# Weight loads of an attention layer put on ScalarE's DMA queue, the filling of three heads changed, and a bank of its own for the last half product

## The chip, the cores and the metric

The kernel runs on one core of one Trainium2 chip. The metric is the device time of one execution in microseconds (us). The number to compare is the median of several executions; the profile is taken from one execution more.

## The reference

The program is a streaming encoder trunk: attention, MLP, a gated linear recurrence, MLP, each with an RMSNorm ahead and a residual add behind, and a last RMSNorm. There are 512 tokens of 1024 channels, all in float32. What the change touches is the attention and the last lines of the last MLP and norm:

```python
qkv = jnp.einsum('bsd,de->bse', h, w_qkv).reshape(B, S, 3, N_HEADS, HEAD_DIM)
...
s = jnp.einsum('bqhd,bkhd->bhqk', q_c, k_band).astype(jnp.float32) * scale + bias
s = jnp.where(key_pos[None, None, None, :] >= 0, s, NEG_INF)
p = jax.nn.softmax(s, axis=-1).astype(v_band.dtype)
return jnp.einsum('bhqk,bkhd->bqhd', p, v_band)
...
return jnp.einsum('bsd,de->bse', o, w_o)
```

There are 16 heads of 64 channels, a band of nine chunks of 64 tokens, and a learned bias by clipped distance. With 512 tokens the band is all earlier tokens and the own chunk.

## The kernel before, in words

**Number format.** Every float32 product is made of three matmuls: high by high, high by low and low by high (`mm3`, L287 to L290). So every operand is split into a high part, a rounded copy, and a low part, the difference.

**Weight units.** Weights come in units of 512 KB, in the order of a list called `plan`. For a unit of the attention, `fetch` (L138) does three things in a row: the DMA into a raw buffer `wr` (L154), the cast of the high part `wh` on ScalarE (ACT, L179), and the subtraction for the low part `wl` on VectorE (DVE, L184). There are three raw buffers, `wr0` to `wr2`, so the DMA of a unit waits until the subtraction of the unit three places earlier has read its buffer. There are five buffers each for `wh` and `wl`. The DMAs stand on SyncE's (SP) queue; only one half of the very first unit is on ACT's. The units are: 0 to 5 for the query and key columns of the heads 0 to 3 (`FIRST`), 6 to 9 for the values of the heads 0 to 7, 10 to 17 for four further pairs of heads, 18 to 21 for the other values, 22 to 25 for the last two pairs, 26 to 33 for the output projection. The MLP's first unit is 34 (`starts[0]`). `want` keeps four units ahead.

**Order of the attention.** Six units of query and key products come first, and among them `flat` (L328): the sum of squares for the norm is cast (`n0a`, L331), summed over the partitions by two matmuls with ones (`n0ss`, L333 and L334) and turned into a scale `n0r` (L336). After that comes a loop over the heads (L674). Each pass holds the scores of head i (`score`, L473: eight matmuls L483 and L484, four passes of the bias and the maximum on DVE L491, four exponentials on ACT L498), the split of the probabilities of head i-2 (`split_p`: `pH` on ACT L549, `pL` on DVE L550), the weighing with the values of head i-3 (`weigh`: matmuls L567 and L568 into the bank `oa`, a copy `ax` on ACT L573, an add `o` on DVE L574), and the division of head i (`divide`: ACT L515, a transpose on DVE L517, and 16 small DMAs L521 that move the blocks `p`, 6 on SP's queue and 10 on GpSimd's, POOL). Four PSUM banks serve scores and `oa` in turn (three for the scores of a head, one for `oa`), so a `weigh` also waits until the maxima of the latest scores have been read. The k parts of a pair of heads go through SP's queue too (L400), and so does each head's bias (L374).

**Filling.** Twice in a pass `fill(n)` puts other TensorE (PE) work between these steps: value products, query and key products of later pairs, and the output projection `wo`. It takes matmuls by a credit of `n`: `FILL` is 11.7 for the heads 0 to 12 and `LATE` is 6.0 after them. What is left is run behind the last head.

**The end.** In `ends` (L1083) the last of the Strassen products, "22", is formed in two parts: `ts=(0,)` into the bank `X[0]`, and `ts=(1,)` into the bank `X[1]`, in two halves of 256 columns, LO and HI. After LO, `X[1]` is read by DVE (L1118), then HI's matmuls follow into the same bank, and DVE reads again. Squares, roots, scales and stores of the rows follow piece by piece (L1094 to L1134).

Of the kernel before, what the change touches and what calls it, by code (L numbers as in the profile page):

```python
# [10 lines left out]
F32 = mybir.dt.float32  # L11
F32R = mybir.dt.float32r
AF = mybir.ActivationFunctionType
ALU = mybir.AluOpType

P = 128
# [3 lines left out]
NH = 16  # L20
# [2 lines left out]
EPS = 1e-6  # L23
NEG = -1e30

FILL, LATE, TURNED = 11.7, 6.0, NH - 2

WARM = 10

# [11 lines left out]
def trunk(ctx: ExitStack, tc: tile.TileContext, xT, cols, gfin, win, wqkv, wo, rwin, rga, rgx, rwo, w1, w2, out):  # L41
    nc = tc.nc
# [9 lines left out]
    def mmp(name):  # L52
        return ps.tile([P, T], F32, name=name, tag="mm")
# [45 lines left out]
    plan = []  # L99
# [9 lines left out]
    def rows(src):  # L109
        return src.rearrange("(k p) c -> p k c", p=P)  # L110
# [14 lines left out]
    def load_up(key, name):  # L125
# [9 lines left out]
        if name == "s1":  # L135
            G.dma_start(four(raw), rows(upper[key]["22"]), accum_op=ALU.add)  # L136

    def fetch():  # L138
        i = state["next"]
        state["next"] += 1  # L140
        kind, nk, key = plan[i]
        H = wsp.tile([P, 1024], F32R, name=f"wh{i}", tag="wh")
        L = wsp.tile([P, 1024], F32R, name=f"wl{i}", tag="wl")
        n, half = 1024, nk
        if kind[:5] == "plain":
            n = nk * sum(src.shape[1] for src in key)
            raw = wraw.tile([P, 1024], F32, name=f"wr{i}", tag=f"wr{state['plain'] % 3}")
            state["plain"] += 1
            rv = raw[:, :n].rearrange("p (k c) -> p k c", k=nk)
            c0 = 0  # L150
            for n_, src in enumerate(key):
                w = src.shape[1]
                queue = nc.scalar if i == 0 and n_ else nc.sync
                queue.dma_start(rv[:, :, c0 : c0 + w], rows(src))  # L154
                c0 += w
        elif kind[0] == "u":
            nk = 4
            following = (key[0], key[1] + 1)
            if kind == "us2":
                raws["us2"] = wraw.tile([P, 1024], F32, name=f"us2_{key[0]}{key[1]}", tag=f"wr{(state['base'] + 2) % 3}")  # L160
                tc.keep_in_program_order(V.tensor_add(raws["us2"], raws["u11"], raws["us1"]))
                raws["us3"] = raws["u11"]
                G.dma_start(four(raws["us3"]), rows(upper[key]["21"]), accum_op=ALU.add)  # L163
            if kind == "us4":
                raws["us4"] = raws["u12"]
                V.tensor_add(raws["us4"], raws["us4"], raws["us2"])
            raw = raws[kind]
        else:
            nk = 2
            following = (key[0], key[1] + 1)  # L170
            raw = raws[{"t1": "12", "t2": "22", "t3": "11", "t4": "21"}.get(kind, kind), half]
            if kind == "t2":
                if key[1] < 3:
                    V.tensor_add(raw, raw, raws["12", half])
                G.dma_start(raws["21", half], raw, accum_op=ALU.add)
            if kind == "t3" and key[1] < 3:
                V.tensor_sub(raw, raws["22", half], raw)
        if i:
            high = S.copy(H[:, :n], raw[:, :n])  # L179
            if kind in ("us1", "us3", "t1", "t4") or kind in ("t2", "t3") and key[1] == 3:  # L180
                tc.keep_in_program_order(high)
        else:
            start_.append(V.tensor_copy(H[:, :n], raw[:, :n]))
        low = V.tensor_sub(L[:, :n], raw[:, :n], f(H[:, :n]))  # L184
        if not i:
            start_.append(low)
        if kind == "plain_":
            state["base"] = state["plain"] % 3
            load_up((nk_layer[i], 0), "11")
            load_up((nk_layer[i], 0), "12")  # L190
        elif kind == "us2" and key[1]:
            load_up(following, "s1")
        elif kind == "us3":
            load_up(following, "11")
        elif kind == "us4":
            load_up(following, "12")
        elif kind == "u22" and key[1]:
            load_up(following, "22")
        elif kind in ("11", "t1", "22", "21", "t2", "t3", "t4") and key[1] == 3:
            hs = slice(half * U, (half + 1) * U)  # L200
            if kind == "t1":
                nc.sync.dma_start(two(raws["11", half]), rows(down[key]["22"][hs]))
                G.dma_start(two(raws["11", half]), rows(down[key]["12"][hs]), accum_op=ALU.add)
            elif kind == "22":
                G.dma_start(raws["22", half], raws["12", half], accum_op=ALU.add)
        elif kind == "t2" and half:
            load_down(following, "12")
        elif kind == "t3" and half:
            load_down(following, "11")
        elif kind == "t4" and half:  # L210
            first_sum(following)
            load_down(following, "22")
            load_down(following, "21")
        state["ready"].append((nk, H[:, :n].rearrange("p (k c) -> p k c", k=nk), L[:, :n].rearrange("p (k c) -> p k c", k=nk)))
# [150 lines left out]
    with ExitStack() as actx:  # L365
# [268 lines left out]
        def step():  # L634
            for item in list(queue):
                if item[0][0] not in "qkv" and item is not queue[0]:
                    break
                try:
                    n = next(item[1])
                except StopIteration:  # L640
                    queue.remove(item)
                    return True
                if n:
                    credit[0] -= n
                    return True
            return False
# [25 lines left out]
            at["w"] = h  # L672

        for i in range(NH + 2):  # L674
            n = FILL if i < 13 else LATE
            if i < NH:
                if 0 < i < NH - 2:
                    bias_of(i + 2)
                if i >= 4:
                    need(f"q{i // 2}")  # L680
                score(i)
                if i == 0:
                    k_out(1, accs[3])
                at["s"] = i
            fill(n)
            if 0 <= i - 2 < NH - 2:
                split_p(i - 2)
            if 0 <= i - 3 < NH - 2:
                weigh_at(i - 3)
            fill(n)  # L690
            if i < NH:
                divide(i)
            if i >= NH:
                split_p(i - 2)
                fill(n)
                weigh_at(i - 2)
# [41 lines left out]
    def mlp(ly, norm):  # L738
        with ExitStack() as mctx:
# [73 lines left out]

            def read(acc, t, c):
                d, r = dt[t, c], (nrq if c else rq)[:, t : t + 1]
                V.scalar_tensor_tensor(d, acc, r, d, ALU.mult, ALU.add)


            a = {}
# [263 lines left out]
            def ends(step, product, X, gfins):  # L1083
                gain = [gfins[:, c] for c in range(2)]

                def store(t, c, queue):
                    queue.dma_start(out[t * P : (t + 1) * P, c * T : (c + 1) * T], dt[t, c])

                tc.keep_in_program_order(S.activation(spare, epsb, AF.Sqrt))
                step("s3", X, False, 2, 1)  # L1090
                for t in range(2):
                    for c in range(2):
                        squares(t, c)
                    V.tensor_add(total(t), total(t), part(t, 1))  # L1094
                    S.activation(total(t), total(t), AF.Sqrt, bias=epsb, scale=1.0 / D)
                    V.reciprocal(total(t), total(t))
                    for c in range(2):
                        V.scalar_tensor_tensor(dt[t, c], dt[t, c], total(t), gain[c], ALU.mult, ALU.mult)
                        store(t, c, nc.sync)
                for t in (2, 3):  # L1100
                    squares(t, 1)
                    V.tensor_scalar(part(t, 1), part(t, 1), 1.0 / D, EPS, ALU.mult, ALU.add)
                    V.tensor_mul(dt[t, 1], dt[t, 1], gain[1])
                product("22", X, False, ts=(0,))
                read(X[0], 2, 0)
                squares(2, 0)
                S.activation(total(2), total(2), AF.Sqrt, bias=part(2, 1), scale=1.0 / D)
                V.reciprocal(total(2), total(2))
# [2 lines left out]
                S.activation(dt[2, 1], dt[2, 1], AF.Copy, scale=total(2))  # L1111
                store(2, 1, nc.scalar)

                d, x, g = dt[3, 0], X[1], gain[0]
                sq = wk.tile([P, T], F32, name="fsq30", tag="nsq", bufs=2)
                for n, c in enumerate((LO, HI)):
                    product("22", X, False, ts=(1,), cols_=c)
                    V.scalar_tensor_tensor(d[:, c], x[:, c], rq[:, 3:4], d[:, c], ALU.mult, ALU.add)  # L1118
                    S.activation(sq[:, c], d[:, c], AF.Square, accum_out=fs[:, 4 * n : 4 * n + 1])
                    if n == 0:  # L1120
                        V.scalar_tensor_tensor(part(3, 1), fs[:, 0:1], 1.0 / D, part(3, 1), ALU.mult, ALU.add)
                        V.tensor_mul(d[:, c], d[:, c], g[:, c])
# [221 lines left out]
```

## Time and profile before

| | |
|---|---|
| median of three executions | 1023.05 us (1020.48 to 1025.93) |
| the profiled execution | 1022.14 us, of which the profile's span is 1020.3 us |
| PE busy | 1005.4 us (99%) |
| DVE busy | 858.2 us (84%) |
| ACT busy | 681.6 us (67%) |
| POOL busy | 170.7 us (17%) |
| largest wait of PE for another engine | 4.5 us, at 185.81 us |
| attention, first score (L483) to last weighing (L568) | 41 to 219 us |

A page of the profile lists the busy time of each engine, its share of the span and its count of instructions. In a row of the timeline stand the start, the duration, the engine, the line, the operation, the tiles as out<-in, shapes and how many; in square brackets stands how long the engine was idle ahead of it, and which instruction released it. PE's matmuls overlap, so their spacing is the difference of two starts. "SPq" is a DMA issue on SP's queue. Of a matmul that stands in a row behind another, the duration is longer than the spacing.

### The profile page before, as it was taken

Reading aid. Unit: us, or ns where it says so; the run is one execution under the profiler, and the core shown is the slowest. Engines: PE = TensorE matmul, PEld = TensorE weight load, DVE = VectorE, ACT = ScalarE, POOL = GpSimd, SP = SyncE. Lnnn points to the kernel's source line nnn. Section 1 sums busy time; section 2 is a strip of 40 time slices with the busy share of each in tenths; the row PEclk is TensorE's granted clock in tenths of the full one; section 3 lists DMA queues with packets and bytes.
Section 4 is the critical chain, followed back from the end, with each engine's and each line's share of the span. In section 5 each row is a group of like instructions: output and inputs, shape, how many; then the busy total and the mean of one; then the engine's idle time right before and its main releaser. Section 6 shows DMA issues by size and latency. Waiting matters only on the chain.

```text
span 1020.3 us, 15680 instructions
## 1 busy us (share of the span) xinstructions
PE 1005.4 (99%) x5650; PEld 880.3 (86%) x5650; DVE 858.2 (84%) x1136; ACT 681.6 (67%) x1032; POOL 170.7 (17%) x280
## 2 busy tenths in 40 slices
PE   9999999899999999999999999999999999999997
PEld 8888888688999999999988788888999999999986
DVE  7798888889799798698698988977699698798687
ACT  7577787656876566576477696546776566566565
POOL 1055454404011011011110000013011111111020
PEclk9999999899999999999999999999999999999999
DMA  8687768648757657746863313196748747737572
GB/s 267 170 236 195 188 172 227 191 136 215 207 128 197 171 131 177 188 105 165 228 121 109 119 63 97 49 277 157 206 86 205 205 83 207 206 63 207 145 153 95
DMA packets 136749, 167.03 MB, mean 164 GB/s; under 512 B 10784, under 2 KB 101536, under 8 KB 136672
## 3 DMA queue, kind: packets, MB, share of 16 engines
q1 hardware_dynamic: 109536, 121.83, 38.8%
q0 software_dynamic: 26560, 43.50, 23.3%
q8 instruction: 44, 0.72, 0.3%
q10 hardware_dynamic: 576, 0.72, 0.2%
q14 instruction: 33, 0.27, 0.1%
HBM read 123.27 MB, written 2.10 MB: 123 GB/s over the span
## 4 chain that ended last, share of the span: by engine, by line
PE 77%; DVE 8%; DMA 5%; ACT 4%; issue 3%; SPq 2%; POOL 1%; DVEq 0%; ACTq 0%
PE m L290 9%; PE m L289 9%; PE m L288 9%; PE x L289 5%; PE x L288 5%; PE x L290 5%; PE y L288 4%; PE y L289 4%; PE y L290 4%; DVE wl L184 2%; DMA wr<-in_wqkv 2%; DMA p<-pt 2%; PE ro L290 1%; PE yb L288 1%; PE ro L289 1%
## 5 line engine op out<-in xcount | busy, mean ns | idle before, releaser
L184 DVE TENSOR_TENSOR wl<-b,wh 128x1024 fp32r<-128x1024 f32 x112 | 135.8, 1222 | 37.2 <-ACT wh L179 37.1
L179 ACT CAST wh<-b 128x1024 fp32r<-128x1024 f32 x112 | 116.9, 1051 | 63.4 <-PE m L289 19.9
L290 PE MATMUL m<-rH,wl 128*128 128x256 f32 x448 | 125.9, 281 | 0.0
L289 PE MATMUL m<-rL,wh 128*128 128x256 f32 x448 | 125.8, 281 | 0.0
L288 PE MATMUL m<-rH,wh 128*128 128x256 f32 x448 | 125.7, 281 | 0.0
L290 PE MATMUL m<-hnH,wl 128*128 128x256 f32 x336 | 95.0, 283 | 0.0
L289 PE MATMUL m<-hnL,wh 128*128 128x256 f32 x336 | 95.0, 283 | 0.0
L288 PE MATMUL m<-hnH,wh 128*128 128x256 f32 x336 | 94.9, 282 | 0.0
L179 ACT CAST wh<-wr 128x1024 fp32r<-128x1024 f32 (+1 forms) x65 | 66.6, 1028 | 36.7 <-PE ro L289 8.5
L184 DVE TENSOR_TENSOR wl<-wr,wh 128x1024 fp32r<-128x1024 f32 (+1 forms) x66 | 78.3, 1191 | 12.3 <-ACT wh L179 11.9
L289 PEld LDWEIGHTS m<-rL,wh 128*128 128x128 f32 x448 | 85.0, 190 | 1.2
L288 PEld LDWEIGHTS m<-rH,wh 128*128 128x128 f32 x448 | 84.8, 189 | 1.0
L290 PEld LDWEIGHTS m<-rH,wl 128*128 128x128 f32 x448 | 84.9, 189 | 0.0
L521 POOL DMA_DIRECT2D p<-pt x140 | 68.7, 499 | 58.0 <-DVE pt L517 34.6
L179 ACT CAST wh<-u 128x1024 fp32r<-128x1024 f32 x56 | 58.2, 1051 | 28.0 <-PE x L290 16.9
L184 DVE TENSOR_TENSOR wl<-u,wh 128x1024 fp32r<-128x1024 f32 x56 | 67.6, 1219 | 2.3 <-ACT wh L179 2.3
L289 PEld LDWEIGHTS m<-hnL,wh 128*128 128x128 f32 x336 | 64.3, 191 | 0.8
L288 PEld LDWEIGHTS m<-hnH,wh 128*128 128x128 f32 x336 | 64.2, 191 | 0.8
L290 PEld LDWEIGHTS m<-hnH,wl 128*128 128x128 f32 x336 | 64.3, 191 | 0.0
L136 POOL DMA_DIRECT2D kept<-in_w x14 | 18.3, 1306 | 272.9 <-DVE t L1284 146.6
L163 POOL DMA_DIRECT2D u<-in_w x14 | 18.4, 1315 | 229.1 <-ACT m L906 122.3
L288 PE MATMUL x<-wh,h 128*128 128x512 f32 (+1 forms) x132 | 51.0, 386 | 0.6 <-DVE d L1118 0.6
(389 smaller groups left out, 2998.9 us busy)
## 6 DMA issues: line engine op xcount, KB each, us to landing
b<-in_w SPq DMA_DIRECT2D x68, 512.0 KB, 5.9
b<-b POOLq DMA_DIRECT2D x36, 512.0 KB, 6.7
kept<-in_w SPq DMA_DIRECT2D x28, 512.0 KB, 4.2
u<-in_w SPq DMA_DIRECT2D x28, 512.0 KB, 6.2
wr<-in_wqkv SPq DMA_DIRECT2D x20, 512.0 KB, 4.8
wr<-in_rwin SPq DMA_DIRECT2D x16, 512.0 KB, 3.7
kept<-in_w POOLq DMA_DIRECT2D x14, 512.0 KB, 6.9
u<-in_w POOLq DMA_DIRECT2D x14, 512.0 KB, 7.7
```

The source lines that it names most:

```text
L136: G.dma_start(four(raw), rows(upper[key]["22"]), accum_op=ALU.add)
L163: G.dma_start(four(raws["us3"]), rows(upper[key]["21"]), accum_op=ALU.add)
L179: high = S.copy(H[:, :n], raw[:, :n])
L184: low = V.tensor_sub(L[:, :n], raw[:, :n], f(H[:, :n]))
L288: PE.matmul(acc, WH, XH, start=start, stop=False, skip_group_check=more)
L289: PE.matmul(acc, WH, XL, start=False, stop=False, skip_group_check=more)
L290: PE.matmul(acc, WL, XH, start=False, stop=stop, skip_group_check=more)
L521: move = queue.dma_start(pt[32 * j : 32 * j + 32, i * 320 : (i + 1) * 320], turned[32 * i : 32 * i + 32, j].rearrange("p s a -> p (s a)"),)
```

## The change

There are three edits.

1. **Loads.** The DMA of a plain unit becomes a function of its own, `load(i)`. For the units 6 to 33 it goes to ACT's queue, and for those units `fetch(i)` issues the load of unit i+1 ahead of its own cast. The loads from unit 34 on stay on SP's queue and are issued in their own `fetch`.
2. **Filling.** `FILL` is 11.2 in place of 11.7, `LATE` is 7.0 in place of 6.0, and `LATE` begins with head 14 in place of head 13.
3. **The end.** The HI half of the last product goes to a fresh bank, `last`. A DVE instruction `rest` adds what `X[1]` holds of the HI half to `d` beforehand. The matmuls of `ts=(0,)` are written ahead of the squares of the rows 2 and 3, and the reading of `X[0]` comes ahead of the last `tensor_mul`.

```diff
-FILL, LATE, TURNED = 11.7, 6.0, NH - 2
+FILL, LATE, TURNED = 11.2, 7.0, NH - 2
...
+    loaded = {}
+
+    def load(i):
+        kind, nk, key = plan[i]
+        n = nk * sum(src.shape[1] for src in key)
+        raw = wraw.tile([P, 1024], F32, name=f"wr{i}", tag=f"wr{state['plain'] % 3}")
+        state["plain"] += 1
+        rv = raw[:, :n].rearrange("p (k c) -> p k c", k=nk)
+        c0 = 0
+        for n_, src in enumerate(key):
+            w = src.shape[1]
+            queue = nc.scalar if i == 0 and n_ or len(FIRST) <= i < starts[0] else nc.sync
+            queue.dma_start(rv[:, :, c0 : c0 + w], rows(src))
+            c0 += w
+        loaded[i] = raw, n
...
         if kind[:5] == "plain":
...
-                queue = nc.scalar if i == 0 and n_ else nc.sync
-                queue.dma_start(rv[:, :, c0 : c0 + w], rows(src))
-                c0 += w
+            for j in range(i, i + 2 if len(FIRST) <= i < starts[0] - 1 else i + 1):
+                if j not in loaded:
+                    load(j)
+            raw, n = loaded.pop(i)
...
-            n = FILL if i < 13 else LATE
+            n = FILL if i < 14 else LATE
...
                 step("s3", X, False, 2, 1)
+                d, g = dt[3, 0], gain[0]
+                rest = V.scalar_tensor_tensor(d[:, HI], X[1][:, HI], rq[:, 3:4], d[:, HI], ALU.mult, ALU.add)
...
-                        V.scalar_tensor_tensor(dt[t, c], dt[t, c], total(t), gain[c], ALU.mult, ALU.mult)
+                        ins = V.scalar_tensor_tensor(dt[t, c], dt[t, c], total(t), gain[c], ALU.mult, ALU.mult)
+                        if t == 1:
+                            after(ins, rest)
                         store(t, c, nc.sync)
+                product("22", X, False, ts=(0,))
                 for t in (2, 3):
                     squares(t, 1)
                     V.tensor_scalar(part(t, 1), part(t, 1), 1.0 / D, EPS, ALU.mult, ALU.add)
-                    V.tensor_mul(dt[t, 1], dt[t, 1], gain[1])
-                product("22", X, False, ts=(0,))
-                read(X[0], 2, 0)
+                    if t == 3:
+                        ins = read(X[0], 2, 0)
+                    mul = V.tensor_mul(dt[t, 1], dt[t, 1], gain[1])
+                after(mul, ins)
...
-                d, x, g = dt[3, 0], X[1], gain[0]
...
-                    product("22", X, False, ts=(1,), cols_=c)
+                    x = mmp("last") if n else X[1]
+                    product("22", (None, x), n == 1, ts=(1,), cols_=c)
                     V.scalar_tensor_tensor(d[:, c], x[:, c], rq[:, 3:4], d[:, c], ALU.mult, ALU.add)
```

The order of the instructions on an engine shows what moves. In it a name ends in a number of its own buffer, and a line of the changed kernel is higher by 10 in the attention. First ACT at the start of the program, before: `wh5` to `wh10` are the casts of the units 5 to 10, `n0a0` is the cast for the norm's sum.

```order
L179 CAST wh5_195<-wr5_197 128x1024
L179 CAST wh6_249<-wr6_251 128x1024
L331 CAST n0a0_322<-n0acc_202 128x512
L179 CAST wh7_267<-wr7_269 128x1024
L336 ACTIVATE n0r_328<-n0ss_321,epsb_94 128x512
L179 CAST wh8_285<-wr8_287 128x1024
L179 CAST wh9_315<-wr9_317 128x1024
L179 CAST wh10_399<-wr10_401 128x1024
```

The same place on ACT in the changed kernel, with the loads of the units 7 to 10 (`L150 DMA wr7` and so on) and two squares of the norm (`n0sq6`, `n0sq7`):

```order
L189 CAST wh5_195<-wr5_197 128x1024
L327 ACTIVATE n0sq6_219<-x1_75 128x512
L327 ACTIVATE n0sq7_222<-x1_75 128x512
L150 DMA wr7_253<-in_wqkv 128x2x512
L189 CAST wh6_249<-wr6_251 128x1024
L150 DMA wr8_271<-in_wqkv 128x2x512
L189 CAST wh7_269<-wr7_253 128x1024
L150 DMA wr9_289<-in_wqkv 128x2x512
L189 CAST wh8_287<-wr8_271 128x1024
L150 DMA wr10_319<-in_wqkv 128x8x128
L189 CAST wh9_317<-wr9_289 128x1024
L341 CAST n0a0_324<-n0acc_202 128x512
```

The cast `n0a0` moved from ahead of `wh7` to behind `wh9`, and the issues of the loads stand between the casts. The two squares, which stood ahead of `wh5`, are behind it now.

Next PE at the start, before; `n0ss` are the two matmuls with ones that need `n0a0` and its low part `n0a1`:

```order
L289 MATMUL qk03_135<-hnL5_89,wh4_182 128x512
L290 MATMUL qk03_135<-hnH5_81,wl4_183 128x512
L333 MATMUL n0ss_321<-n0a0_322,ones_93 128x512
L334 MATMUL n0ss_321<-n0a1_323,ones_93 128x512
L288 MATMUL qk00_132<-hnH6_82,wh5_195 128x512
L289 MATMUL qk00_132<-hnL6_90,wh5_195 128x512
```

And in the changed kernel, where `v00` is the first value product:

```order
L299 MATMUL qk03_135<-hnL7_91,wh5_195 128x512
L300 MATMUL qk03_135<-hnH7_83,wl5_196 128x512
L343 MATMUL n0ss_323<-n0a0_324,ones_93 128x512
L298 MATMUL v00_427<-wh6_249,hnH0_76 128x512
L299 MATMUL v00_427<-wl6_250,hnH0_76 128x512
L300 MATMUL v00_427<-wh6_249,hnL0_84 128x512
L298 MATMUL v00_427<-wh6_249,hnH1_77 128x512
L299 MATMUL v00_427<-wl6_250,hnH1_77 128x512
L344 MATMUL n0ss_323<-n0a1_325,ones_93 128x512
```

The two matmuls for the norm moved from behind 72 query and key matmuls to behind all 96, the second of them behind five value matmuls more. From there to the first score 72 value matmuls stand, so 77 in all, where before there were 56.

Last, SP near the end of the attention, before: `p11` and `p12` are the block moves of the heads 11 and 12, `bias` the biases, `wr30` to `wr34` the loads of weight units:

```order
L521 DMA p11_1877<-pt11_1982 32x320 x6
L374 DMA bias14_2000<-in_win 128x256
L154 DMA wr30_2044<-in_wo 128x4x256
L154 DMA wr31_2100<-in_wo 128x4x256
L521 DMA p12_2007<-pt12_2115 32x320 x6
L374 DMA bias15_2133<-in_win 128x256
L154 DMA wr32_2249<-in_wo 128x4x256
L154 DMA wr33_2333<-in_wo 128x4x256
L154 DMA wr34_2408<-in_w1 128x8x128
```

And in the changed kernel:

```order
L384 DMA bias14_1959<-in_win 128x256
L410 DMA kh70_1993<-kH7_1989 64x512 x2
L531 DMA p11_1849<-pt11_1941 32x320 x6
L410 DMA kh71_1995<-kH7_1989 64x512 x2
L410 DMA kl70_1994<-kL7_1990 64x512 x2
L410 DMA kl71_1996<-kL7_1990 64x512 x2
L384 DMA bias15_2104<-in_win 128x256
L531 DMA p12_1966<-pt12_2086 32x320 x6
L150 DMA wr34_2408<-in_w1 128x8x128
```

The loads `wr30` to `wr33` no longer stand between the block moves. In all, 28 loads left SP's queue and 28 were added to ACT's.

Of the filling, counted in PE's order: between the last score of head 14 and the first matmul of `oa` of head 11 there were 9 matmuls of `wo`, and there are 28 now; between the scores of head 13 and `oa` of head 10 there were 9, and there are 18. Between the scores and the `oa` of head 11 there were 99 filling matmuls, and there are 127.

More of the change, by code (lines that the diff above doesn't have):

```diff
@@ L145, in fetch @@
         if kind[:5] == "plain":
[L146 to L152, printed above, removed]
-                queue = nc.scalar if i == 0 and n_ else nc.sync
-                queue.dma_start(rv[:, :, c0 : c0 + w], rows(src))
-                c0 += w
+            for j in range(i, i + 2 if len(FIRST) <= i < starts[0] - 1 else i + 1):
+                if j not in loaded:
+                    load(j)
+            raw, n = loaded.pop(i)
         elif kind[0] == "u":
@@ L815, in read @@
                 d, r = dt[t, c], (nrq if c else rq)[:, t : t + 1]
-                V.scalar_tensor_tensor(d, acc, r, d, ALU.mult, ALU.add)
+                return V.scalar_tensor_tensor(d, acc, r, d, ALU.mult, ALU.add)
             a = {}
```

## The prediction

> **What bounds the kernel now.** I read the page first, then the waits of PE, the timeline around the longest of them, and the busy time by window.
>
> ```profile
> PE 1005.4 (99%) x5650; PEld 880.3 (86%) x5650; DVE 858.2 (84%) x1136; ACT 681.6 (67%) x1032; POOL 170.7 (17%) x280
> ```
>
> PE is busy for 1005.4 of 1020.3 us. Where no matmul is dropped, as here, a change gains at most what PE stands still or runs slowly. The waits of PE (total us, times, longest):
>
> ```profile
> PE oa L567 <- DVE mx L491: 4.5, 1, 4.5
> PE oa L567 <- DVE o L574: 0.9, 1, 0.9
> PE x L288 <- DVE d L1118: 0.6, 1, 0.6
> PE s L483 <- DMA kl<-kL: 0.5, 1, 0.5
> ```
>
> The first is as long as the others together and more. The timeline around it:
>
> ```profile
> 185.58 0.39 PE L289 MATMUL wo<-oL,wh 128*128 128x512 f32 x1
> 185.81 0.39 PE L290 MATMUL wo<-oH,wl 128*128 128x512 f32 x1
> 190.66 0.58 PE L567 MATMUL oa<-pL,v 128*128 128x256 f32 x1 [4.46 <-DVE mx L491]
> 175.36 3.88 SPq L521 DMA_DIRECT2D p<-pt  x6
> 179.90 1.15 SPq L154 DMA_DIRECT2D wr<-in_wo  x2
> 184.37 1.05 ACT L179 CAST wh<-wr 128x1024 fp32r<-128x1024 f32 x1 [4.58 <-DMA wr<-in_wo]
> 185.45 1.23 DVE L184 TENSOR_TENSOR wl<-wr,wh 128x1024 fp32r<-128x1024 f32 x1 [2.12 <-ACT wh L179]
> 187.27 1.48 DVE L550 TENSOR_TENSOR pL<-p,pH 128x1280 fp32r<-128x1280 f32 x1
> 188.66 1.22 DVE L184 TENSOR_TENSOR wl<-wr,wh 128x1024 fp32r<-128x1024 f32 x1
> 189.80 0.29 DVE L491 CUSTOM_DVE_ANT_0 p<-s,bias 128x128 f32<-128x128 f32 x1
> 190.21 0.40 DVE L491 CUSTOM_DVE_ANT_0 p<-s,bias 128x256 f32<-128x256 f32 x1
> ```
>
> Read backwards: `oa` of head 11 needs the bank that DVE empties at 190.6 (two passes L491); DVE came late because it stood 2.12 us for `wh`, and ACT stood 4.58 us for a weight load. That load was issued at 179.90, behind six block moves that held SP's queue for 3.88 us. PE had run out of filling at 185.81. What followed (us; busy of PE, PEld, DVE, ACT, POOL; granted clock; DMA share; GB/s):
>
> ```profile
> 185.81:189.02 3.21, 0.39 (x2) 0.00 (x0) 3.21 (x5) 2.95 (x7) 1.56 (x4) 1.00 0.81 208
> 189.02:190.66 1.64, 0.00 (x0) 0.00 (x0) 1.57 (x6) 1.62 (x6) 0.48 (x2) 0.50 1.02 352
> 190.66:195.86 5.20, 5.20 (x17) 4.62 (x18) 5.09 (x10) 4.92 (x12) 1.52 (x4) 0.50 0.64 178
> ```
>
> PE's clock fell to half at 189.02, 2.8 us after the last matmul (185.81 + 0.39), and 5.20 us of matmuls ran at half speed, a loss of 2.6 us. The place costs 4.5 + 2.6 = 7.1 us.
>
> **The change part by part.** The sum is made against the profiled execution, 1022.14 us, which lies 0.9 below the median of the three runs, inside their spread.
>
> *The stall, -7.1.* Two covers come at once. The loads 30 to 33 leave SP's queue and are issued a unit sooner, so ACT's 4.58 us for the load shrink or go. And between the scores of head 14 and this `oa` stand 28 filling matmuls in place of 9; at the spacing 185.81 - 185.58 = 0.23 us the 19 more are 4.3 us, against a wait of 4.46. Either nearly does it alone, so I take all 4.5, and without the idleness no half clock (2.6). If the first fails, 0.2 is left; if neither works, all 7.1.
>
> *The other waits, -1.6.* The 0.9 for `o` comes one head earlier, where 9 fillers become 18 (9 x 0.23 = 2.0 us of cover): gone. The 0.5 for `kl` ahead of the first score is gone, since 21 value matmuls more (4.8 us) stand ahead of it. At the end PE's 0.6 goes, but DVE sets that end:
>
> ```profile
> 1010.40 0.68 DVE L1103 TENSOR_TENSOR d<-d,gfins 128x512 f32<-128x512 f32 x1
> 1011.00 0.75 DVE L816 SCALAR_TENSOR_TENSOR d<-x,rq,d 128x512 f32<-128x512 f32 x1
> 1014.19 0.48 DVE L1118 SCALAR_TENSOR_TENSOR d<-x,rq,d 128x256 f32<-128x256 f32 x1
> ```
>
> The multiplication (1011.00 - 1010.40 = 0.60) moves behind the read, and `rest`, like the last row at most 0.48, is new ahead of it: -0.1 to -0.2; I take -0.2, between 0 and -0.6.
>
> *The start, +2.3.* This is the part that speaks against the change.
>
> ```profile
> 17.35 2.01 ACT L179 CAST wh<-wr 128x1024 fp32r<-128x1024 f32 x2
> 19.27 0.61 ACT L331 CAST n0a<-n0acc 128x512 fp32r<-128x512 f32 x1
> 21.59 0.40 PE L333 MATMUL n0ss<-n0a,ones 128*128 128x512 f32 x1
> 22.41 0.39 PE L288 MATMUL qk<-hnH,wh 128*128 128x512 f32 x1
> 27.86 0.39 PE L288 MATMUL v<-wh,hnH 128*128 128x512 f32 x1
> wr<-in_wqkv SPq DMA_DIRECT2D x3, 512.0 KB, 4.6
> L154 ACTq DMA_DIRECT2D wr<-in_wqkv x1: 456/456/456, 1.2 to 1.2; - x1
> ```
>
> (The last two: landing time of the loads issued from 20 to 26 us, and the one issue from ACT's queue, in ns.) In the order after, `n0a0` stands on ACT behind `wh9`, `wh9` needs load 9, load 9's issue stands behind `wh7`, and `wh7` needs load 7. The issue of load 7 follows the same work as `wh6` before, which began at about 18.4 (17.35 + half of 2.01): say 18.5. It lands at 18.5 + 4.6 = 23.1; load 9, issued as `wh7` starts, lands at 27.7; a cast (1.0) and `n0a0` (0.6) end at 29.3. PE is at `n0ss` by 27.86 - 0.82 = 27.04, 0.82 being what the two matmuls for the norm took before (22.41 - 21.59) and no longer take ahead of it. The wait is 29.3 - 27.0 = 2.3. With landings of 4.0 it is 1.1, with 5.3 and an issue of 0.46 in front of either load 4.6; I keep 0.9 to 5. What is queued behind: the second `n0ss` and all value products.
>
> *The middle, +1.0.* ACT takes up 28 issues; at 0.46 us each 12.8 us in all.
>
> ```profile
> 50.00:100.00 50.00, 50.00 (x245) 42.58 (x244) 43.50 (x86) 39.43 (x85) 26.61 (x57) 1.00 0.79 213
> 100.00:150.00 50.00, 50.00 (x253) 42.53 (x252) 42.55 (x84) 40.14 (x81) 23.94 (x52) 1.00 0.69 184
> 64.86 1.48 DVE L550 TENSOR_TENSOR pL<-p,pH 128x1280 fp32r<-128x1280 f32 x1
> 73.18 0.28 PE L567 MATMUL oa<-pL,v 128*128 128x256 f32 x1
> 176.76 1.49 DVE L550 TENSOR_TENSOR pL<-p,pH 128x1280 fp32r<-128x1280 f32 x1 [0.60 <-DMA kl<-kL]
> 179.03 0.39 PE L567 MATMUL oa<-pL,v 128*128 128x256 f32 x1 [0.94 <-DVE o L574]
> ```
>
> ACT is idle for 10.6 and 9.9 of 50 us here and PE not at all, so most issues hide. Head 0's probabilities are split 6.8 us before use (73.18 - 64.86 - 1.48), head 10's 0.8 (179.03 - 176.76 - 1.49). A late cast of up to 0.5 then costs something at heads like the latter only, and `FILL` is lower by 0.5 a time. I take 1.0 from a possible 0 to 4 (half a microsecond at eight heads).
>
> Sum: 1022.14 - 7.1 - 1.6 + 2.3 + 1.0 = 1016.7. The same difference, -5.4, from the median gives 1017.6. I take the middle, **1017.2**.
>
> **The rivals.**
>
> *A: the start wait trips the clock, 1019.8.* The clock fell after 2.8 us of idleness at the stall; a wait of 2.3 is near. Half clock would cost 2.6 more, as it did there. Against it: the waits of 0.9 and less did not trip it, and my 2.3 is uncertain both ways. [...]
>
> *B: the stall only moves, 1021 to 1024.5.* Late loads may be late because the DMA engines are full, whichever queue issues them. For it: the DMA share is 0.81 and 1.02 in the two windows of the stall. Then `wh` stays late, the filling covers half to none, and 3.5 to 7.1 come back. Against: the 3.88 us of block moves stood just ahead of the issue on the same queue, and the loads now start a unit sooner. [...]
>
> *C: slower, about 1031.* An issue on ACT waits for the `wl` of three units before, and behind it stand the exponentials, `pH` and `ax`.
>
> ```profile
> SPq L154 <- DVE wl L184: 189.4, 41, 35.8
> ```
>
> On SP's queue that wait was 189.4 us over 41 issues, 4.6 each, and held nothing but moves; on ACT it holds the softmax. If it holds ACT longer than the slack (about 1 to 2 us at the later heads), PE stops at most heads: 14 heads x 1 us = 14 us, so 1017 + 14 = 1031. Against it: on SP the issue came early and so waited long; on ACT it stands right ahead of a cast, by when the buffer has mostly been read.
>
> *D: the start wait hides, 1014.5.* If load 7 lands by 21 us, the 2.3 and part of the 1.0 go.
>
> **How the numbers follow.** Forecast 0.50 (its own range 1014.3, with the start at 0.9, no wait in the middle and 0.4 more at the end, to 1021), A 0.15, B 0.15, C 0.08, D 0.12. From 1013 to 1024.5 leaves out C, the tail of D and the top of B and A, under 0.2. Measurements of this kernel tell about 0.5% (5.1 us) from no change, so faster means below 1017.9: six tenths of the forecast's 0.50 (0.30), all of D (0.12), a bit of A and B (0.06): 0.48. Slower is above 1028.2: C and a little of B with a worse start, 0.09. The rest, 0.43, is within 0.5%.
>
> **What would show it.** In the profile of the changed kernel: no wait of PE over 1 us between 180 and 200 us, and a granted clock of 1.00 there; the issue of loads on ACT next to casts, with ACT idle for `wr` under 2 us near 184; a wait of PE for `n0a` near 27 us of 1 to 5 us, with the clock at 1.00 (forecast) or 0.50 behind it (A); waits of PE for `pL` or `mx` that sum to some 1 us (forecast) or recur at most heads (C). The prediction is wrong if the start wait is absent or over 5, if the stall stands elsewhere at over 3 us, or if PE stops at head after head.

## The result, and the profile after

The changed kernel is slower: 1033.41 us median of six executions (1031.25 to 1036.34), against 1023.01 us for the kernel before (1020.48 to 1025.93, six executions). The ratio is 1.0113, with a 95% interval of 1.0097 to 1.0129. The forecast was 1017.2, between 1013.0 and 1024.5. The span of the profiled execution is 1031.6 us, 11.3 more than before.

PE's busy time hardly moved. First the page, then the waits of PE in the changed kernel:

```profile
PE 1006.1 (98%) x5650; PEld 879.9 (85%) x5650; DVE 859.7 (83%) x1137; ACT 681.8 (66%) x1032; POOL 171.0 (17%) x280
```

```profile
PE s L493 <- DMA p<-pt: 7.9, 1, 7.9
PE oa L577 <- DVE o L584: 1.8, 3, 1.1
PE wo L298 <- ACT oH L588: 1.8, 1, 1.8
PE n0ss L343 <- ACT n0a L341: 1.6, 1, 1.6
PE s L493 <- DMA kl<-kL: 1.6, 1, 1.6
```

The 4.5 us at head 11's weighing and the 0.6 for `d` at the end are gone. In their place stand 7.9 us ahead of the scores of head 12, and three single waits of 1.6 to 1.8 (the row for `o` sums three short ones). Around the largest, the timeline of SP and PE after:

```profile
151.32 2.72 SPq L681 DMA_DIRECT2D h<-in_xT  x6
154.95 5.02 SPq L531 DMA_DIRECT2D p<-pt  x6
162.35 0.81 SPq L681 DMA_DIRECT2D h<-in_xT  x2
163.26 3.08 SPq L410 DMA_DIRECT2D kh<-kH  x4
166.43 2.89 SPq L410 DMA_DIRECT2D kl<-kL  x4
174.84 0.44 PE L493 MATMUL s<-kl,q 128*128 128x128 f32 x1 [7.94 <-DMA p<-pt]
```

and SP at the same place before:

```profile
154.01 2.47 SPq L400 DMA_DIRECT2D kh<-kH  x4
156.58 2.46 SPq L400 DMA_DIRECT2D kl<-kL  x4
159.14 3.87 SPq L671 DMA_DIRECT2D h<-in_xT  x8
```

The `h<-in_xT` rows are the reload of x for the residual, eight DMAs of 256 KB that the code issues behind head 7's weighing (`weigh_at`). Before, they stood behind the moves of the k part of heads 12 and 13; now they stand ahead of them. The trace names a block move as the releaser of the stall, but what head 12's scores need are the k moves, whose last issue ends at 169.3. From issue to landing they took much longer too. DMA issues from 150 to 165 us before, with KB each and the median time to landing:

```profile
kl<-kL SPq DMA_DIRECT2D x4, 128.0 KB, 2.4
p<-pt SPq DMA_DIRECT2D x9, 40.0 KB, 2.7
```

and from 150 to 175 us after:

```profile
kl<-kL SPq DMA_DIRECT2D x4, 128.0 KB, 7.2
p<-pt SPq DMA_DIRECT2D x11, 40.0 KB, 6.1
```

The windows after show the stall and the half clock that it leaves behind (columns as in the prediction):

```profile
170.00:172.00 2.00, 0.00 (x0) 0.00 (x0) 2.00 (x3) 1.96 (x4) 0.00 (x0) 0.95 1.07 293
172.00:174.80 2.80, 0.00 (x0) 0.00 (x0) 1.30 (x2) 0.00 (x0) 0.00 (x0) 0.50 0.71 159
174.80:178.00 3.20, 3.16 (x10) 2.90 (x11) 1.84 (x4) 1.05 (x1) 0.00 (x0) 0.50 0.41 115
```

At the start, the chain of casts stands as the prediction read it from the order; ACT's and PE's timelines after:

```profile
21.80 1.06 ACT L189 CAST wh<-wr 128x1024 fp32r<-128x1024 f32 x1 [1.29 <-DMA wr<-in_wqkv]
27.25 1.04 ACT L189 CAST wh<-wr 128x1024 fp32r<-128x1024 f32 x1 [1.95 <-DMA wr<-in_wqkv]
28.20 0.61 ACT L341 CAST n0a<-n0acc 128x512 fp32r<-128x512 f32 x1
28.87 0.50 PE L343 MATMUL n0ss<-n0a,ones 128*128 128x512 f32 x1 [1.59 <-ACT n0a L341]
```

### The profile page after: what moved, and what is told of

The parts are those of the page before. It is cut to its first block, busy times and chain, and to the rows that moved or that the text cites. A ratio compares the mean times of both kernels' runs of the same rounds, so it can differ in the third digit from the quotient of the medians.

```text
span 1031.6 us, 15664 instructions
## 1 busy us (share of the span) xinstructions
PE 1006.1 (98%) x5650; PEld 879.9 (85%) x5650; DVE 859.7 (83%) x1137; ACT 681.8 (66%) x1032; POOL 171.0 (17%) x280
## 4 chain that ended last, share of the span: by engine, by line
PE 76%; DMA 7%; DVE 7%; ACT 6%; issue 2%; SPq 1%; DVEq 0%; POOL 0%; ACTq 0%
PE m L300 8%; PE m L298 8%; PE m L299 8%; PE x L299 5%; PE x L300 5%; PE x L298 5%; PE y L299 4%; PE y L298 4%; PE y L300 4%; DMA p<-pt 2%; DMA wr<-in_wqkv 2%; DVE wl L194 2%; ACT p L508 2%; DMA kl<-kL 1%; PE ro L300 1%
## 5 line engine op out<-in xcount | busy, mean ns | idle before, releaser
L531 POOL DMA_DIRECT2D p<-pt x140 | 68.7, 499 | 38.4 <-DMA p<-pt 11.2
L299 PE MATMUL y<-wl,hs 128*128 128x512 f32 x128 | 50.1, 391 | 0.6 <-DVE wl L194 0.6
```

The lines of the kernel that those rows point to most:

```text
L299: PE.matmul(acc, WH, XL, start=False, stop=False, skip_group_check=more)
L531: move = queue.dma_start(pt[32 * j : 32 * j + 32, i * 320 : (i + 1) * 320], turned[32 * i : 32 * i + 32, j].rearrange("p s a -> p (s a)"),)
```

## The experiments

Three theories were on the table. **Theory 1:** the loads on ACT's queue cause the loss. **Theory 2:** the lower filling number brings head 12 to PE before its k part is split. **Theory 3**, formed after eight runs from the order on SP's queue: the lower filling number lets the reload of x slip ahead of the k moves. The runs were made in four sets, 1 to 4, 5 to 8, 9 to 12 and 13 to 15. In each set the kernel before ran beside the others on the same chip; its medians were 1022.93, 1022.75, 1022.58 and 1022.73 us, and each ratio is to these. A wait read from one profile is less sure than a median: the kernel before and run 3 have the same attention, as have runs 4 and 12, and runs 10 and 15, and the same wait differs between the two by 1.5, 1.1 and 1.6 us.

**1. The loads alone**, filling and end as before.

```diff
+            queue = nc.scalar if i == 0 and n_ or len(FIRST) <= i < starts[0] else nc.sync
...
+            for j in range(i, i + 2 if len(FIRST) <= i < starts[0] - 1 else i + 1):
+                if j not in loaded:
+                    load(j)
```

> The loads' edit alone (ACT's queue, one unit sooner), with the old filling and the old end. Theory 1: the loads cause the new stall of 7.9 us ahead of the scores of head 12, since they change what stands ahead of the k moves on SP's queue and whose landing SP waits for; then this kernel shows that stall again, at 5 us or more, and takes 1028 to 1034 us. Theory 2: the lower filling number brings head 12 to PE before its k part is there; then this kernel has no stall over 2 us at head 12 and takes 1018 to 1024 us.

1026.52 us, ratio 1.0035 (1.0020 to 1.0049). Neither theory's numbers hold: there is no wait at head 12, as theory 2 has it, but the time is above its range, and the loss is a third of the whole. The stall near the end of the attention did not go, though the loads had left SP's queue; its 4.4 us stand at head 10's weighing now:

```profile
PE oa L577 <- DVE o L584: 6.4, 4, 4.4
PE n0ss L343 <- ACT n0a L341: 1.5, 1, 1.5
```

**2. The filling alone.**

```diff
-FILL, LATE, TURNED = 11.7, 6.0, NH - 2
+FILL, LATE, TURNED = 11.2, 7.0, NH - 2
...
-            n = FILL if i < 13 else LATE
+            n = FILL if i < 14 else LATE
```

> The filling numbers alone, loads and end as before. Theory 1: no stall at head 12; the stall of 4.5 us at head 11's weighing shrinks, and the time is 1016 to 1023 us. Theory 2: the stall of head 12's scores for k is here, at 5 us or more, and the time is 1025 to 1034 us.

1024.48 us, ratio 1.0011 (1.0000 to 1.0022). The wait at head 12 is there without any change to the loads, though the time is just below theory 2's 1025:

```profile
PE s L483 <- DMA kl<-kL: 5.2, 1, 5.2
PE oa L567 <- DVE o L574: 2.2, 2, 1.8
```

The old stall of 4.5 us is gone here, so the total moves little: the stall has changed its place. Theory 1 falls as the sole cause.

**3. The end alone** (all of the change in `read` and `ends`, among it the bank).

```diff
-                    product("22", X, False, ts=(1,), cols_=c)
+                    x = mmp("last") if n else X[1]
+                    product("22", (None, x), n == 1, ts=(1,), cols_=c)
```

> The end alone. Both theories: 1022.8 to 1023.0 us, 0 to 0.2 us less than before, since DVE and not PE sets the end; PE's wait of 0.6 us for d is gone. If the fresh bank gave what PE waited, 1022.3 or less.

1021.93 us, ratio 0.9990 (0.9980 to 1.0001), not told from no change. The median lies in the branch in which the fresh bank pays, but the trace does not bear that out. The wait of 0.6 for `d` is gone from PE's list, yet from DVE's read of `X[0]` to the last instruction it takes as long as before:

```profile
1012.22 0.75 DVE L816 SCALAR_TENSOR_TENSOR d<-x,rq,d 128x512 f32<-128x512 f32 x1 [0.17 <-PE x L290]
```

1021.5 - 1012.22 = 9.3 us here, 1020.3 - 1011.00 = 9.3 before. DVE sets this end, as the prediction had it.

**4. One unit sooner, on SP's queue.** As run 1, with

```diff
-            queue = nc.scalar if i == 0 and n_ or len(FIRST) <= i < starts[0] else nc.sync
+            queue = nc.scalar if i == 0 and n_ else nc.sync
```

> One unit sooner, but on SP's queue as before; old filling and old end. Theory 1, if ACT's queue is what hurts: no stall at head 12, 1017 to 1024 us. Theory 1, if the earlier issue itself hurts (SP then waits for an older buffer ahead of the moves and of k): the moves come late, with PE waits over 3 us, and 1026 us or more. Theory 2: like the kernel before, 1020 to 1024 us.

1022.06 us, ratio 0.9987 (0.9977 to 0.9996), slightly better than the kernel before. Beside run 1, this says that it is the queue and not the sooner issue that costs. The queue here includes what it does to the order of everything else: by their traces PE's order in run 4 is that of the kernel before up to the end of the attention, and in run 1 it is not.

**5. The changed kernel with FILL 11.7.**

```diff
-FILL, LATE, TURNED = 11.2, 7.0, NH - 2
+FILL, LATE, TURNED = 11.7, 7.0, NH - 2
```

> The changed kernel with one number put back: FILL 11.7 in place of 11.2; LATE 7 from head 14, the loads and the end as changed. Theory 2 (less filling ahead of head 12 lets its scores reach PE before its k part has landed): the stall at head 12 goes or falls under 2 us, and the time falls by 6 to 10 us, to 1023 to 1027 us. Theory 1 (the loads delay k by themselves): the stall stays at 5 us or more, and the time stays over 1029 us.

1029.26 us, ratio 1.0059 (1.0037 to 1.0081). The wait at head 12 is gone, but 4.2 us are won and not 6 to 10, since another stall stands at head 12's weighing:

```profile
PE oa L577 <- DVE o L584: 9.1, 5, 5.2
PE wo L298 <- ACT oH L588: 2.2, 2, 2.0
```

**6. LATE 7 from head 14 alone**, loads and end as before.

```diff
-FILL, LATE, TURNED = 11.7, 6.0, NH - 2
+FILL, LATE, TURNED = 11.7, 7.0, NH - 2
...
-            n = FILL if i < 13 else LATE
+            n = FILL if i < 14 else LATE
```

> The kernel before with LATE 7 from head 14 and nothing else. If only the lower FILL harmed: no stall at head 12's scores, PE's wait at head 11's weighing falls from 4.5 us to under 2 us, and the time is 1015 to 1020 us. If the filling of the last heads only moves the stall on: a wait of 3 us or more after 190 us, and 1021 to 1024 us.

1025.42 us, ratio 1.0023 (1.0011 to 1.0034). A miss for both branches: the stall at head 11's weighing is 5.4 us and not under 2, it has not moved to another head, and the time is above 1024 us. In PE's order 12 filling matmuls stand between head 14's scores and this weighing instead of 9 (28 in the changed kernel), and ACT again stood for the load, in its timeline:

```profile
185.54 1.05 ACT L179 CAST wh<-wr 128x1024 fp32r<-128x1024 f32 x1 [4.90 <-DMA wr<-in_wo]
```

**7. FILL 11.2 alone.**

```diff
-FILL, LATE, TURNED = 11.7, 6.0, NH - 2
+FILL, LATE, TURNED = 11.2, 6.0, NH - 2
```

> The kernel before with FILL 11.2 and nothing else. Theory 2: the stall of about 5 us for k ahead of head 12's scores, as in the run of the filling alone; the time is 1022 to 1030 us, by whether the stall at head 11's weighing stands beside it. Rival: LATE and its switch at head 14 made that stall; then none over 2 us is there at head 12, and the time is 1020 to 1024 us.

1026.13 us, ratio 1.0032 (1.0021 to 1.0043), with a wait of 5.2 us at head 12. So it is this number, not LATE, that makes the wait. In the order on SP's queue, all kernels with 11.2 so far have the reload ahead of the k moves, and of those with 11.7 the kernels before and 1, 3, 4, 5 and 6 have it behind them; in run 8, next, one of its eight DMAs goes ahead. The changed kernel (`h0`, `h1` the reload, `kh6`, `kl6` the k part of heads 12 and 13):

```
L531 DMA p8_1484<-pt8_1567 32x320 x6
L681 DMA h0_1767<-in_xT 128x512 x4
L681 DMA h1_1768<-in_xT 128x512 x2
L531 DMA p9_1592<-pt9_1681 32x320 x6
L681 DMA h1_1768<-in_xT 128x512 x2
L410 DMA kh60_1786<-kH6_1782 64x512 x2
```

The code issues the reload behind head 7's weighing, and the k part comes out of the filling; less filling ahead turns the two round. That gave theory 3.

**8. The loads on ACT's queue, not sooner.** As run 1, with

```diff
-            for j in range(i, i + 2 if len(FIRST) <= i < starts[0] - 1 else i + 1):
+            for j in range(i, i + 1):
```

> The loads on ACT's queue, each issued in its own fetch and not a unit sooner; old filling and old end. If the queue is the cost (27 issues in front of ACT's own work, and the norm's cast behind them): the same as the loads' edit with one unit sooner, 1025 to 1028 us, with the wait of 1.5 us for the norm's cast. If the sooner issue is the cost: 1021 to 1024 us. If the sooner issue helps on ACT's queue: over 1029 us, with casts that wait for their loads.

1029.90 us, ratio 1.0069 (1.0042 to 1.0095), over run 1 by 3.4 us. In its timeline ACT stands 3.19 us for a weight load at 24.55 and 3.11 us at 165.96. With the loads on ACT's queue the sooner issue helps: it takes back 3.4 us of what the queue costs.

**9. The reload behind the k moves, in the changed kernel.** The reload waits for a flag and is issued from `k_out`:

```diff
+        def reload():
+            if owed and 6 in placed:
+                owed.clear()
+                residual("h")
+                for k in range(KT):
+                    after(nc.sync.dma_start(hT[k], xT[k * P : (k + 1) * P, :]), placed[6])
...
             if h == 7:
-                residual("h")
-                for k in range(KT):
-                    nc.sync.dma_start(hT[k], xT[k * P : (k + 1) * P, :])
+                owed.append(h)
+                reload()
```

> The changed kernel with the reload of x (2 MB in eight DMAs on SP's queue) put behind the k moves of heads 12 and 13, as it stands in the kernel before; the order on PE, ACT and DVE is unchanged. Theory 3: the lower FILL let this reload slip ahead of the k moves, where it fills the DMA engines and holds SP's queue, and that makes the 7.9 us at head 12; then that stall falls to 3 us or less and the time to 1023 to 1028 us, by whether the stall turns up at a later head. Theory 1 or 2 without the reload (the k part is projected or split too late): the stall stays at 5 us or more, and the time over 1030 us.

1027.55 us, ratio 1.0052 (1.0033 to 1.0071): 5.9 us less than the changed kernel. The expectation took the order on PE, ACT and DVE as unchanged, and by the traces it is not. Up to head 12's scores PE's order differs by 3 matmuls only (10 of the last query product ahead of them, not 13). Behind them, 26 filling matmuls in place of 18 stand between the scores of head 13 and the weighing of head 10, and 12 in place of 28 between the scores of head 14 and the weighing of head 11. So the 5.9 us are what the moved reload and the new order give together. There is no wait at head 12; the k moves land in 2.5 us again, on SP's timeline and in the list of DMA issues:

```profile
157.82 2.59 SPq L410 DMA_DIRECT2D kh<-kH  x4
160.51 2.48 SPq L410 DMA_DIRECT2D kl<-kL  x4
163.09 5.02 SPq L422 DMA_DIRECT2D h<-in_xT  x8
kl<-kL SPq DMA_DIRECT2D x4, 128.0 KB, 2.5
```

For the wait at head 12 this is what theory 3 says; run 10 tests it with PE's order kept. Part of the stall came back later, at head 10's weighing and head 14's scores:

```profile
PE oa L587 <- DVE pL L570: 3.5, 2, 2.6
PE s L503 <- DMA kl<-kL: 3.0, 1, 3.0
```

**10. The same in the filling alone** (runs 2 and 9 together).

> The filling numbers alone, with the same reload put behind the k moves. Theory 3: the 5.2 us at head 12's scores fall to 2 us or less; the time is 1017 to 1021 us, unless the stall at head 11's weighing is back (then 1021 to 1024). Theory 2: the 5.2 us stay, and the time stays near 1024.5 us.

1022.82 us, ratio 0.9999 (0.9987 to 1.0010), 1.7 us less than run 2. PE's order is here the same as in run 2 up to the end of the attention, so this pair shows the place of the reload by itself. The wait at head 12 fell from 5.2 to 0.8 us, as theory 3 has it:

```profile
PE s L493 <- issue: 0.8, 1, 0.8
```

So theory 3 holds. The time came out in the branch with the stall back, spread over the weighings of heads 11 to 13 at 1.2 to 1.5 us each. So the new filling, without its accident, gains nothing.

**11. The loads of units 6 to 9 back on SP's queue, in the changed kernel.**

```diff
-            queue = nc.scalar if i == 0 and n_ or len(FIRST) <= i < starts[0] else nc.sync
+            queue = nc.scalar if i == 0 and n_ or len(FIRST) + 4 <= i < starts[0] else nc.sync
```

> The changed kernel with the loads of the units 6 to 9 back on SP's queue; the norm's two matmuls stand behind 72 query and key matmuls again. The forecast's start: PE's wait of 1.6 us for the norm's cast goes, and the first scores come as early as before; the time falls by 1.5 to 3 us, to 1030.5 to 1032 us. Rival: the later stall at head 12 takes it back, since it hangs on the loads and not on PE; then 1033 us or more.

1030.38 us, ratio 1.0068 (1.0048 to 1.0089), 3.0 us less. The wait for the norm's cast is gone, that for k ahead of head 12 stands at 7.6.

**12. Sooner on SP's queue with the new end.** Runs 3 and 4 together.

> Loads one unit sooner on SP's queue, with the new end, and the filling as before. If the two gains seen one by one add up (1.0 and 0.9 us): 1020.5 to 1021.5 us. If the end's gain was a matter of the stall at head 11 and not of the end: 1021.8 to 1022.8 us.

1021.56 us, ratio 0.9987 (0.9977 to 0.9997), just between the two branches; by the ratio the end adds nothing to run 4. These two are the best kernels of the study, 0.1% ahead of the kernel before.

**13. Both mendings in the changed kernel** (runs 9 and 11 together).

> The changed kernel with both mendings: the reload of x behind the k moves, and the loads of the units 6 to 9 on SP's queue. If the two losses stand apart and add (5.9 and 3.0 us seen one by one): 1024 to 1025.5 us, about 2 us above the kernel before, the rest being the loads 10 to 33 on ACT's queue. If a stall takes up what is gained: 1026 us or more.

1025.04 us, ratio 1.0027 (1.0015 to 1.0039). The two add, as expected: 8.4 us less than the changed kernel.

**14. All of the change but ACT's queue**, with the reload behind the k moves (run 9, and the queue as in run 4).

> All of the change but ACT's queue: loads one unit sooner on SP's queue, the new filling, the new end, and the reload behind the k moves. If ACT's queue is what is left of the loss: 1018.5 to 1021.5 us, less than the kernel before. If the new filling costs as much as it gives whatever the queue: 1021.5 to 1023 us.

1023.32 us, ratio 1.0003 (0.9994 to 1.0012), just above the second branch. 1.7 us less than run 13: that is what the loads 10 to 33 on ACT's queue cost, again with the order that comes with them. No wait of PE is over 1.8 us here, but there are more of them:

```profile
PE oa L587 <- DVE o L594: 4.6, 4, 1.8
```

**15. Filling and end with the reload behind the k moves, loads as before** (run 10 and run 3 together).

> The new filling and the new end with the reload behind the k moves, and the loads as before, not sooner. If the gain of the end (0.7 to 1.0 us) adds to the filling: 1021.7 to 1022.2 us. If loading one unit sooner is what the new filling needs: no better than 1022, and over the run with sooner loads by 1 us or more.

1022.18 us, ratio 0.9999 (0.9988 to 1.0009). Sooner loads are not what the new filling lacks. The wait at head 12 is 2.4 us here and 0.8 in run 10, with the same attention.

## Why the prediction was wrong

The loss of 10.4 us splits by runs 9, 13 and 14: 5.9 for the place of the reload with the order that went with it, 2.5 for the first four loads (3.0 with the reload still misplaced), 1.7 for the other loads on ACT's queue, and 0.3 that no run tells from nothing. These are differences of medians and good to 1 or 2 us; the executions of run 9 alone spread from 1024.54 to 1033.51.

Set beside the forecast's sum, -5.4, the miss is 15.8 us. The stall and the other waits were to give -8.7, and all of the change but ACT's queue, with the reload behind the k moves (run 14), gave +0.3. The middle was +1.0 and came to 7.6, the 5.9 and the 1.7. The start was nearly right. So two steps failed.

**The first step that failed: "the middle, +1.0".** It priced the lower `FILL` as part of a microsecond of late casts. What it changes is the order on SP's queue at head 8 to 10: 2 MB of reload ahead of the k moves. Runs 2 and 7 show the wait of 5.2 us from the filling number alone, and runs 9 and 10 take all or most of it away by moving the reload back. The prediction weighed the order of SP near the end of the attention only; the row that mattered stands a few rows earlier on the same queue. In the changed kernel the wait is 7.9 and not 5.2. PE came to head 12 4.1 us later than in run 7 (166.9 against 162.8), but the first `kl` move was issued 4.8 us later (166.4 against 161.6) and the moves took 1.7 us more to land (7.2 against 5.5). One of the reload's DMAs waited there for an earlier weight load as well (the row below, from SP's waits between 150 and 182 us). That the k part was split later is not the reason: `kL` was done at 160.7 us, well ahead of its issue, and at 160.1 in run 9, which has no wait at head 12.

```profile
SPq L681 <- DMA wr<-in_wo: 2.4, 1, 2.4
```

**The second step that failed: "the stall, -7.1", taken as a gain of the whole kernel.** The stall at head 11's weighing did go in the changed kernel, with 28 matmuls of cover. But "either nearly does it alone" was not so: the loads alone left 4.4 us at head 10's weighing (run 1), LATE alone 5.4 at head 11's (run 6, where the cover is 12 and not 28). The mechanism named for it, ACT idle for a load behind SP's block moves, was there again in run 6, at 4.90 us. And wherever the stall went, PE waited elsewhere: between 160 and 222 us its waits sum to over 5 us in every kernel of this study, 5.8 in the kernel before and 5.5 in run 14. The half clock does not always follow a wait: the granted clock was 1.00 behind the 2.71 us of run 4 (185.3 to 191 us) and behind the 2.56 and 2.72 us of run 13 (175 to 200 us), and in run 15, behind 2.37 us, no matmul of 512 columns from 150 to 200 us took over 0.40 us, where in run 12 it took 0.63 at half clock. The forecast had no term for a stall that moves. Its rival B did, by name, held at 0.15; its mechanism, full DMA engines that make loads late, fits the k moves (`kl` took 7.2 us to land in the changed kernel, at a DMA share of 0.91 from 163.26 to 174.84 us, and 2.4 in the kernel before, at 0.83 from 154.00 to 161.50) but is not shown for the weight loads.

**The start, +2.3: right in mechanism, a little large as a wait, small as a price.** The wait was 1.6 us; the casts fell at 21.80 and 27.25, where 23.1 and 27.7 were reckoned. Taking the four loads off ACT's queue gave 2.5 to 3.0 us, so about one more than the wait itself came out of it; in run 11 the wait at head 4's scores fell as well, from 1.6 to 0.6 us. **Rival A** did not come: behind the wait of 1.6 us the granted clock stayed at 1.00 (28.87 to 35.00 us); the last section has a wait of that length behind which it fell.

**The other waits, -1.6: mostly not.** The end gave nothing that can be measured, as the prediction's -0.2 said, and the wait for `kl` ahead of the first score went. The wait for `o` went at head 10 and came back at other heads: 0.9 us in one place became 1.8 in three. New are 1.6 us for k ahead of head 4 and 1.8 for `oH` at the close of the attention, which the sum did not have.

**Rival C** gave 1031 us, near the result, by chance: PE did not stop at every head. The loads on ACT's queue cost 1.7 us beyond the start, not 14. Runs 1 and 4 show no gain from ACT's queue: with the same sooner loads, SP's queue gave 1022.06 us and ACT's 1026.52, 4.5 us more.

What stays open: why the stall of the last heads always finds another place, and how much of each loss is the moved DMAs and how much the order of the other engines that changed with them. Nothing was tried that shortens the chain from scores to weighing itself.

## What to carry to other kernels

A number that sets how much filling stands between steps also sets which DMA comes first on a queue; compare the whole queue before and after, not the place that the number is meant for (here 2 MB of reload came ahead of the k moves, and PE waited 5.2 us in run 7). A stall taken away at one head of a serial chain is a gain only if the next head has slack; add up the waits of the whole stage, not the one wait (here 5.8 us before and 5.5 in run 14). And an issue moved to another engine takes a place in that engine's order: look at what is then behind it (here the norm's cast, for which PE waited 1.6 us). An experiment that moves one DMA can reorder other engines too, as run 9 did; compare their orders before its time is put down to the DMA.

## What the runs showed of the hardware

In these runs the length of one wait did not tell whether PE's clock would fall. In run 4 PE stood 2.71 us ahead of head 14's scores, and the clock stayed at 1.00:

```profile
182.00:185.30 3.30, 0.59 (x3) 0.18 (x2) 2.68 (x7) 2.27 (x3) 2.41 (x6) 1.00 0.84 268
185.30:188.00 2.70, 2.70 (x13) 2.14 (x14) 2.30 (x7) 2.04 (x6) 2.70 (x6) 1.00 0.96 276
```

In run 12 (sooner on SP's queue with the new end) it stood 1.58 us at the same place, and the clock then went to half for about 3 us while PE was at work:

```profile
182.00:184.80 2.80, 1.22 (x7) 0.69 (x5) 2.49 (x7) 2.01 (x3) 2.14 (x5) 1.00 0.66 198
184.80:186.00 1.20, 1.20 (x7) 0.90 (x8) 1.20 (x5) 0.00 (x0) 1.20 (x4) 1.00 1.05 346
186.00:189.00 3.00, 3.00 (x8) 2.31 (x9) 2.60 (x4) 2.37 (x7) 2.33 (x5) 0.51 1.08 305
```

Here a shorter wait cost the clock and a longer one did not. In the stretch with the wait PE was busy for 1.22 of 2.80 us in run 12 and for 0.59 of 3.30 in run 4. Behind the 1.59 us at the start of the changed kernel the clock stayed at 1.00. What decides it is not shown by these runs.

The half clock lasted 3.4 us in run 12 (186.0 to 189.4), 6.8 in the kernel before (189.02 to 195.86) and 6.8 in the changed one (171.8 to 178.6). In run 11 PE's matmuls of 512 columns stood 0.43 us apart from 174.5 to 178.3 us, against 0.23 ahead of the stall.

And where the reload of 2 MB was issued ahead of them, the `kl` moves of 128 KB took 5.5 us to land (run 7) and 7.2 (the changed kernel); where it was issued behind them, 2.4 (the kernel before and run 10), but 4.3 in run 5. In run 8, with one of its eight DMAs ahead, they took 5.9. So the place of the reload alone does not set that time.
